# A decoder trunk on one core: decay scores in four-way steps, attention heads in pairs, small columns in the first block, memory tokens split four tiles after their load

## The chip, the core and the metric

The kernel runs on one core of one Trainium2 chip. The core has TensorE (PE, matrix products into PSUM), VectorE (DVE), ScalarE (ACT), GpSimd (POOL) and SyncE (SP, which issues the transfers here). Weights come from the chip's main memory through the core's 16 DMA engines. The metric is the device time of one execution in microseconds: the median of several runs. One further execution was profiled, and all rows below are from it.

## What is computed

One layer over 256 tokens of width 2048, in float32. Cut to what matters here:

```python
h = rmsnorm(x, norm_gain); z = h @ w_in            # one projection, split into all of the below
# A) gated linear attention, 4 heads, keys 128 wide, values 256 wide, chunks of 64
gk_log = log_sigmoid(gdown @ w_gk_up + b_gk) / 16   # gdown: 16 columns of z
b = cumsum(gk_log)                                  # log decay, per key channel
scores[i, j] = sum_d q[i, d] * k[j, d] * exp(b[i, d] - b[j, d])      for j <= i
o_a = rmsnorm(scores @ v + carried state) * silu(ggate)
# B) forgetting attention, 8 heads of 64; c = cumsum(log_sigmoid(flogit + b_f)), 8 columns of z
p = softmax(q.k / 8 + c_t - c_s, for s <= t);       o_b = (p @ v) * silu(fgate)
# C) attention into 256 memory tokens, 4 heads of 128, from rmsnorm(mem) @ w_mem_kv
o_c = softmax(q.mem_k / sqrt(128)) @ mem_v * silu(mgate)
y = sum over the branches of sigmoid(merge_b) * (o_b @ w_branch_b)
out = rmsnorm(x + y @ w_out, final_gain)
```

## The kernel before

**The main stream.** All weights are cut into 34 blocks of 512 columns in the order in which they are used. A block has 16 k-tiles of 128 rows. Float32 products are made from split operands: `split_w` (L123 to 125) casts a raw tile to a rounded `hi` on ScalarE (L124) and subtracts on VectorE to get `lo` (L125), and the activations are split in the same way (L256, L257). A block is then either `natural` (tokens in rows, L166 to L168: three products of 512 columns per k-tile and token half) or `transposed` (channels in rows, L187 with 512 columns and L189 with 256, four such pairs per k-tile). Weights arrive in quarters of four k-tiles (1 MB) in `raw` tiles, of which there are three; `hi` and `lo` have four buffers of two k-tiles each.

**The order of the work.** The orders of TensorE and of SP are those of the program. The orders on VectorE, ScalarE and GpSimd are made by a planner when the kernel is built; it takes work that its own costs say is ready, the weight splits first (`tc.high_priority(AHEAD)`), and else by place in the program. The attention work is written as generators: after each k-tile (in `transposed` after each of the four column groups, which comes to as many) `pull()` lets the side lane and the main lane go on; a `yield n` means n such tiles until the next piece. The main lane holds, one after another, `small_and_norm`, `gla_decay`, `gla_scores`, `gla_out`, `fox` and `memory`; the side lane loads and splits the memory tokens (`load_mem`).

**The first block** (`first_w`, L279 to 300) loads activations and weights in small pieces and is `transposed` with one k-tile at a time into four banks of the `att` pool (128 x 512 floats, four banks; `acc` is the other pool of four).

**The small columns.** The 16 gate columns and the 8 forget columns (`wsm`, L340) are laid into 128-column tiles `zs` after the first block, and sixteen products of 512 columns (L386) follow in `small_and_norm`, within the second block.

**The decay scores.** exp(b_i - b_j) is made finite by a reference point between j and i. For each level s in 64, 32, 16, 8, 4, 2, 1 a 128-token tile is cut into blocks of s; the keys of an even block and the queries of the odd block behind it are scaled against the last row of the even block (`prep`: two differences L453 and L454, one exponential L455, two products L457 and L460). Eight products of 64 columns per level (L495) go to one bank, are multiplied by a mask (L497) and added into the scores `gA` (L500); the next level follows 11 tiles later. The diagonal comes first from products of all keys with all queries (L477) and a scaled identity. The products across the two token tiles are in L485.

**The heads of the forgetting attention** run through `staged(8, (scores, trans, values), (0, 2, 3), 3)`: one head per stage every three tiles. `values` (L589 to 596) multiplies with 64 columns of weights, for even heads into rows 0 to 63 of a bank and for odd heads into rows 64 to 127; two banks are held for all eight heads.

Of the kernel before, what the change touches and what calls it, by code (L numbers as in the profile page):

```python
# [16 lines left out]
P = 128  # L17
S = 256
# [34 lines left out]
LEVEL_GAP = 11  # L53
N_WARM = 8
LEVELS = (64, 32, 16, 8, 4, 2, 1)
# [4 lines left out]
def body(ctx, tc, xT, memT, xn, memn, wall, wsm, wup, cst, fgain, out):  # L60
# [93 lines left out]
    def h_of(h, kt):  # L154
        return h[kt // 4][:, kt % 4]
# [116 lines left out]
    def load_mem():  # L272
        for g in range(4):
            m12.append(new_h("m12_", g))
            raw = wpool.tile([P, 4, S], F32, tag="raw", name=nm("raw"), bufs=3)
            load_split(memT, "m12_", C_MGAIN, g, m12[g], raw, slice(0, 4))
            yield 6

    def first_w():  # L279

        wb = w_block()
        for g in range(4):
# [5 lines left out]
            for s in range(2):  # L288
# [28 lines left out]
    def scale_T(r, row):  # L317
        nc.vector.tensor_tensor(out=r, in0=r, in1=row.unsqueeze(1).to_broadcast([P, 4, S]), op=ALU.mult)
        return r
# [19 lines left out]
    wsr = cpool.tile([P, KT, 24], F32, name="wsr")  # L339
    nc.sync.dma_start(wsr, wsm)  # L340
    wup_s = cpool.tile([16, 512], F32, name="wup_s")
    nc.sync.dma_start(wup_s, wup)

    gmask = cpool.tile([P, len(LEVELS), 64], F32, name="gmask")
    nc.gpsimd.memset(gmask, QS)
    for li, s in enumerate(LEVELS):
        nb = 64 // s
        mk_ = gmask[:, li, :].rearrange("p (b s) -> p b s", s=s)
        nc.gpsimd.affine_select(out=mk_, in_=mk_, pattern=[[-2 * s, nb], [0, s]],
                                compare_op=ALU.is_ge, fill=0.0, base=0, channel_multiplier=1)  # L350
        nc.gpsimd.affine_select(out=mk_, in_=mk_, pattern=[[2 * s, nb], [0, s]],
                                compare_op=ALU.is_ge, fill=0.0, base=s - 1, channel_multiplier=-1)
    gdiag = cpool.tile([P, P], F32, name="gdiag")
    nc.vector.tensor_scalar(gdiag, ident, QS, None, ALU.mult)
# [8 lines left out]

    zs = []
    for g in range(2):
        z0 = a4([P, 8, P], F32)
        nc.gpsimd.memset(z0, 0.0)
        ws = a4([P, 8, P], F32R)
        wr = wsr[:, 8 * g:8 * g + 8, :]
        nc.vector.tensor_copy(ws, z0)  # L370
        for (a, b, wdt) in ((0, 0, 16), (32, 16, 8)):
            nc.vector.tensor_copy(ws[:, :, a:a + wdt], wr[:, :, b:b + wdt])
            nc.vector.tensor_tensor(out=ws[:, :, 64 + a:64 + a + wdt], in0=wr[:, :, b:b + wdt],
                                    in1=ws[:, :, a:a + wdt].bitcast(F32), op=ALU.subtract)
        zs.append(ws)
    sm = cpool.tile([64, S], F32, name="sm")

    def small_and_norm():
# [5 lines left out]
        sp = att()  # L384
        for kt in range(KT):
            MM(sp, lhsT=zs[kt // 8][:, kt % 8, :], rhs=h_of(x12, kt).rearrange("p a s -> p (a s)"),  # L386
               start=(kt == 0), stop=(kt == KT - 1))
        yield from norm
        yield from row_of(xcol, xrow)
        scale_T(G["q"], xrow)  # L390
        scale_T(G["k"], xrow)
        nc.scalar.copy(sm, sp[0:64, S:])
        nc.vector.tensor_tensor(out=sm, in0=sp[0:64, :S], in1=sm, op=ALU.add)
        nc.vector.tensor_tensor(out=sm, in0=sp[64:128, :S], in1=sm, op=ALU.add)
# [47 lines left out]
    def gla_scores():  # L442
# [3 lines left out]

        def prep(s):
            nb = 1024 // (2 * s)
            Bv = gB.rearrange("p (b u s) -> p b u s", u=2, s=s)
            E = a4([P, 1024])  # L450
            Ev = E.rearrange("p (b u s) -> p b u s", u=2, s=s)
            ref = Bv[:, :, 0, s - 1:s].to_broadcast([P, nb, s])
            nc.vector.tensor_tensor(out=Ev[:, :, 0, :], in0=ref, in1=Bv[:, :, 0, :], op=ALU.subtract)  # L453
# [475 lines left out]
```

## Time and profile before

| | |
|---|---|
| median of 3 runs | 824.55 us (824.29 to 824.95) |
| the profiled execution | 824.89 us, of it the span 823.2 us |
| granted TensorE clock, mean | 0.997 |
| busy: PE, PEld, DVE, ACT, POOL | 98%, 83%, 60%, 50%, 2% |
| transfers | 157.15 MB, 191 GB/s on average |

The span runs from the first to the last instruction. Busy shares are averages over stages with different loads. Products are pipelined, so the duration of one (0.39 us for 512 columns) is longer than the distance from one start to the next (0.23 us), and what work costs TensorE is read from starts. A float32 product of the attention work, whose operands are not split, runs as two passes and counts twice in the number of instructions.

### The profile page before, as it was taken

How to read it: one execution, taken by the hardware profiler on the slowest of the kernel's cores; microseconds unless marked ns; L12 is line 12 of the kernel's file. 1: busy time of each engine (PE TensorE's matmuls, PEld its weight loads, DVE VectorE, ACT ScalarE, POOL GpSimd, SP SyncE). 2: the span in 40 equal slices, each digit the busy share in tenths (PEclk: the TensorE clock that was granted, in tenths of full speed). 3: DMA queues.
4: the chain of work that ended last, by engine and by line, in shares of the span. 5: the costliest groups of instructions: out<-in, count | busy, mean ns of one | idle time of the engine just before them, and what ended most of it. 6: DMA issues, size and time to landing. Idle time of an engine off the chain costs nothing.

```text
span 823.2 us, 10033 instructions
## 1 busy us (share of the span) xinstructions
PE 809.6 (98%) x3958; PEld 679.4 (83%) x3958; DVE 497.6 (60%) x657; ACT 408.4 (50%) x547; POOL 15.4 (2%) x36
## 2 busy tenths in 40 slices
PE   8999999999999999999999999999999999999995
PEld 7888888888888778888888888888888888888885
DVE  6755988875647667567445744475446544566833
ACT  7746755743454456455444444444444444445611
POOL 4000100000000000000000000000000000000000
PEclk9999999999999999999999999999999999999998
DMA  8943466844534344445555545554555455576803
GB/s 302 385 176 125 155 228 230 300 158 169 189 140 168 108 148 154 148 160 199 182 187 199 205 170 192 200 204 167 191 205 202 166 195 205 199 266 249 307 0 103
DMA packets 27359, 157.15 MB, mean 191 GB/s; under 512 B 3216, under 2 KB 4640, under 8 KB 10416
## 3 DMA queue, kind: packets, MB, share of 16 engines
q1 hardware_dynamic: 27040, 156.48, 53.3%
q8 instruction: 31, 0.51, 0.2%
q14 instruction: 16, 0.13, 0.0%
q10 hardware_dynamic: 144, 0.02, 0.0%
q0 software_dynamic: 128, 0.02, 0.0%
HBM read 154.39 MB, written 2.10 MB: 190 GB/s over the span
## 4 chain that ended last, share of the span: by engine, by line
PE 90%; DVE 3%; DMA 2%; ACT 2%; issue 1%; SPq 1%; POOL 0%; DVEq 0%; ACTq 0%; POOLq 0%
PE acc L166 18%; PE acc L168 18%; PE acc L167 18%; PE acc L187 12%; PE acc L189 6%; PE acc L822 4%; PE acc L821 4%; PE acc L820 4%; DMA raw<-wall 1%; PE att L495 1%; DMA raw<-memT 1%; PE att L187 1%; DVE lo L125 1%; ACT hi L124 1%; PE att L593 1%
## 5 line engine op out<-in xcount | busy, mean ns | idle before, releaser
L125 DVE TENSOR_TENSOR lo<-raw,hi 128x1024 fp32r<-128x1024 f32 (+2 forms) x269 | 321.0, 1203 | 248.4 <-ACT hi L124 248.0
L124 ACT CAST hi<-raw 128x1024 fp32r<-128x1024 f32 (+2 forms) x269 | 275.3, 1035 | 291.1 <-PE acc L168 215.2
L166 PE MATMUL acc<-hi,x 128*128 128x512 f32 x544 | 215.3, 396 | 0.0
L168 PE MATMUL acc<-hi,x 128*128 128x512 f32 x544 | 212.0, 390 | 0.0
L167 PE MATMUL acc<-lo,x 128*128 128x512 f32 x544 | 211.8, 389 | 0.0
L187 PE MATMUL acc<-x,hi 128*128 128x512 f32 x384 | 137.2, 400 | 1.1 <-ACT a L327 1.1
L168 PEld LDWEIGHTS acc<-hi,x 128*128 128x128 f32 x544 | 102.1, 188 | 21.7
L166 PEld LDWEIGHTS acc<-hi,x 128*128 128x128 f32 x544 | 102.2, 188 | 21.2 <-issue 0.5
L167 PEld LDWEIGHTS acc<-lo,x 128*128 128x128 f32 x544 | 102.2, 188 | 20.5
L189 PE MATMUL acc<-x,lo 128*128 128x256 f32 x384 | 107.3, 280 | 0.0
L187 PEld LDWEIGHTS acc<-x,hi 128*128 128x128 f32 x384 | 72.1, 188 | 18.1 <-ACT a L327 1.6
L189 PEld LDWEIGHTS acc<-x,lo 128*128 128x128 f32 x384 | 72.4, 189 | 0.3
L166 PE MATMUL acc<-hi,oT 128*128 128x512 f32 x128 | 49.8, 389 | 0.0
L167 PE MATMUL acc<-lo,oT 128*128 128x512 f32 x128 | 49.8, 389 | 0.0
L168 PE MATMUL acc<-hi,oT 128*128 128x512 f32 x128 | 49.8, 389 | 0.0
L820 PE MATMUL acc<-hi,a 128*128 128x512 f32 x96 | 37.5, 391 | 0.0
L822 PE MATMUL acc<-hi,a 128*128 128x512 f32 x96 | 37.4, 389 | 0.0
L821 PE MATMUL acc<-lo,a 128*128 128x512 f32 x96 | 37.4, 389 | 0.0
L167 PEld LDWEIGHTS acc<-lo,oT 128*128 128x128 f32 x128 | 24.0, 188 | 5.0
L168 PEld LDWEIGHTS acc<-hi,oT 128*128 128x128 f32 x128 | 24.0, 188 | 5.0
L166 PEld LDWEIGHTS acc<-hi,oT 128*128 128x128 f32 x128 | 24.0, 188 | 5.0
L187 PE MATMUL att<-x,hi 128*128 128x512 f32 x64 | 23.4, 406 | 0.5 <-ACT hi L124 0.5
(215 smaller groups left out, 781.3 us busy)
## 6 DMA issues: line engine op xcount, KB each, us to landing
raw<-wall SPq DMA_DIRECT2D x132, 1024.0 KB, 4.7
a<-xn SPq DMA_DIRECT2D x8, 512.0 KB, 8.5
raw<-wall SPq DMA_DIRECT2D x4, 512.0 KB, 7.2
raw<-memT SPq DMA_DIRECT2D x4, 512.0 KB, 4.2
raw<-memn SPq DMA_DIRECT2D x4, 512.0 KB, 4.6
out<-a SPq DMA_DIRECT2D x8, 256.0 KB, 3.3
raw<-wall SPq DMA_DIRECT2D x7, 256.0 KB, 4.9
a<-xT SPq DMA_DIRECT2D x8, 128.0 KB, 4.2
```

The source lines that it names most:

```text
L124: nc.scalar.copy(hi, src)
L125: nc.vector.tensor_tensor(out=lo, in0=src, in1=hi.bitcast(F32), op=ALU.subtract)
L166: MM(ps[t], lhsT=h1, rhs=hi, start=(kt == first), stop=False)
L167: MM(ps[t], lhsT=h1, rhs=lo, start=False, stop=False)
L168: MM(ps[t], lhsT=h2, rhs=hi, start=False, stop=(kt == last))
L187: MM(ps[c], lhsT=hi[:, cs_], rhs=hk.rearrange("p a s -> p (a s)"), start=(kt == 0), stop=False, skip_group_check=True)
L189: MM(ps[c][:, :S], lhsT=lo[:, cs_], rhs=hk[:, 0, :], start=False, stop=(kt == KT - 1), skip_group_check=True)
L495: MM(ps[:, e, :], lhsT=E[:, e * P:(e + 1) * P], rhs=Q[:, e, :], start=True, stop=True)
L593: MM(o, lhsT=fv[:, 0, hs], rhs=pt[:, :S], start=True, stop=False, skip_group_check=True)
L820: MM(ps, lhsT=h1, rhs=hi, start=(kt == 0), stop=False)
L821: MM(ps, lhsT=h1, rhs=lo, start=False, stop=False)
L822: MM(ps, lhsT=h2, rhs=hi, start=False, stop=(kt == KT - 1))
```

## The change

- `gla_scores` has steps of 32, 8 and 2 in place of seven levels. In a step a block of 4s tokens is cut into four parts; each part of keys is scaled against its own end, and for each of the first three parts the later queries of the block are scaled against that end: (3+2+1) x 32 = 192 columns a tile. So a step takes two levels' worth of pairs, with eight products of 192 columns over four banks, and its results are copied into `gA` under a mask (`copy_predicated`) and not added. A last step of the same size takes neighbours (64 columns) and, with the plain queries (128 columns), the diagonal. Steps are 18 tiles apart. Queries get their factor QS when they are scaled by `xrow`.
- `fox` takes two heads at a time: the values of a pair go to one bank of their own, with the passes of the two heads side by side, and the stages are written out with two or three tiles between.
- The small columns are loaded and laid out behind the first group of the first block, and their products stand in that block behind the second, third and fourth group, into a bank of `acc`. The copy of zeros moves to GpSimd.
- The memory tokens of a group are split four tiles after their transfer is issued; the next group still follows six tiles after it.
- The warm-up has six products, not eight.

```diff
-LEVEL_GAP = 11
-N_WARM = 8
-LEVELS = (64, 32, 16, 8, 4, 2, 1)
+STEP_GAP = 18
+N_WARM = 6
+STEPS = (32, 8, 2)
+Q_OFF = (0, 96, 160)
+Q_N = 192
...
             raw = wpool.tile([P, 4, S], F32, tag="raw", name=nm("raw"), bufs=3)
-            load_split(memT, "m12_", C_MGAIN, g, m12[g], raw, slice(0, 4))
-            yield 6
+            nc.sync.dma_start(raw, memT[:, 4 * g:4 * g + 4, :])
+            yield 4
+            for k in range(4):
+                kt = 4 * g + k
+                split_x(m12[g], raw[:, k, :], k, cs[:, C_MGAIN + kt:C_MGAIN + kt + 1])
+            yield 2
...
+    def small_w():
+        nc.sync.dma_start(wsr, wsm)
+        for g in range(2):
+            z0 = a4([P, 8, P], F32)
+            nc.gpsimd.memset(z0, 0.0)
+            ws = a4([P, 8, P], F32R)
+            wr = wsr[:, 8 * g:8 * g + 8, :]
+            nc.gpsimd.tensor_copy(ws, z0)
+            for (a, b, wdt) in ((0, 0, 16), (32, 16, 8)):
+                nc.vector.tensor_copy(ws[:, :, a:a + wdt], wr[:, :, b:b + wdt])
+                nc.vector.tensor_tensor(out=ws[:, :, 64 + a:64 + a + wdt], in0=wr[:, :, b:b + wdt],
+                                        in1=ws[:, :, a:a + wdt].bitcast(F32), op=ALU.subtract)
+            zs.append(ws)
+    sp = acc()
+    def small_mm(kts):
+        for kt in kts:
+            MM(sp, lhsT=zs[kt // 8][:, kt % 8, :], rhs=h_of(x12, kt).rearrange("p a s -> p (a s)"),
+               start=(kt == 0), stop=(kt == KT - 1))
...
+            if g == 0:
+                small_w()
+            else:
+                small_mm(range(0 if g == 1 else 4 * g, 4 * g + 4))
...
         def prep(s):
...
+            E = a4([P, 1024])
+            Bv = gB.rearrange("p (b s) -> p b s", s=s)
+            nc.vector.tensor_tensor(out=E.rearrange("p (b s) -> p b s", s=s),
+                                    in0=Bv[:, :, s - 1:s].to_broadcast([P, 1024 // s, s]), in1=Bv,
+                                    op=ALU.subtract)
             nc.scalar.activation(E, E, AF.Exp, scale=1.0 / 16)
             nc.vector.tensor_tensor(out=E, in0=E, in1=gkf, op=ALU.mult)
+            for half in range(2):
+                Q = a4([P, 4, Q_N])
+                for b in range(3):
+                    w, nb = (3 - b) * s, 32 // s
+                    end = blocks(gB, half, 4 * s)[:, :, (b + 1) * s - 1:(b + 1) * s]
+                    nc.vector.tensor_tensor(
+                        out=of_q(Q, b, s), in0=later(gB, half, b, s),
+                        in1=end.rearrange("p (e b) s -> p e b s", e=4).to_broadcast([P, 4, nb, w]),
+                        op=ALU.subtract)
+                nc.scalar.activation(Q, Q, AF.Exp, scale=1.0 / 16)
+                for b in range(3):
+                    nc.vector.tensor_tensor(out=of_q(Q, b, s), in0=of_q(Q, b, s),
+                                            in1=later(gqf, half, b, s), op=ALU.mult)
+                Qs.append(Q)
+            return E, Qs
...
-        for c in range(2):
-            ps = att()
-            for e in range(4):
-                sl = slice((4 * c + e) * P, (4 * c + e + 1) * P)
-                MM(ps[:, e * P:(e + 1) * P], lhsT=gkf[:, sl], rhs=gqf[:, sl], start=True, stop=True)
...
-            yield 3
-        nxt = prep(LEVELS[0])
+        nc.gpsimd.memset(gA, 0.0)
+        yield 6
+        nxt = prep(STEPS[0])
         yield 8
...
+        for li in range(len(STEPS) + 1):
+            E, Qs = nxt
+            if li < len(STEPS):
+                nxt = prep(STEPS[li + 1]) if li + 1 < len(STEPS) else prep_pairs()
+            for c in range(4):
+                ps = att()[:, :2 * Q_N].rearrange("p (a b) -> p a b", a=2)
+                for j in range(2):
+                    e = 2 * c + j
+                    MM(ps[:, j, :], lhsT=E[:, e * P:(e + 1) * P], rhs=Qs[c // 2][:, e % 4, :],
+                       start=True, stop=True)
...
+                for dst, mask, src in parts:
+                    nc.vector.copy_predicated(
+                        dst, mask.bitcast(U32).unsqueeze(1).to_broadcast(list(src.shape)), src)
+            yield STEP_GAP
...
-            o = po[h // 4][64 * (h % 2):64 * (h % 2) + 64, (h // 2) % 2, :]
-            MM(o, lhsT=fv[:, 0, hs], rhs=pt[:, :S], start=True, stop=False, skip_group_check=True)
-            MM(o[:, P:], lhsT=fv[:, 1, hs], rhs=pt[:, S:], start=False, stop=True, skip_group_check=True)
...
+        def values(p):
+            po = att()
+            for a, b, j, sl in ((0, S, 0, slice(0, S)), (P, S, 1, slice(S, 3 * P))):
+                for e in range(2):
+                    h = 2 * p + e
+                    MM(po[64 * e:64 * e + 64, a:b], lhsT=fv[:, j, h * 64:(h + 1) * 64], rhs=pts[h][:, sl],
+                       start=(j == 0), stop=(j == 1), skip_group_check=True)
+            nc.scalar.copy(ob[:, p, :], po[:, :S])
+        for k in range(6):
+            if k >= 2:
+                values(k - 2)
+                yield 2
+            if 1 <= k < 5:
+                for e in range(2):
+                    trans(2 * (k - 1) + e)
+                yield 2
+            if k < 4:
+                for e in range(2):
+                    scores(2 * k + e)
+                yield 3
```

More of the change, by code (lines that the diff above doesn't have):

```diff
@@ L315, in plain_T, with scale_T @@
         return r
-    def scale_T(r, row):
-        nc.vector.tensor_tensor(out=r, in0=r, in1=row.unsqueeze(1).to_broadcast([P, 4, S]), op=ALU.mult)
+    def scale_T(r, row, by=1.0):
+        nc.vector.scalar_tensor_tensor(out=r, in0=r, scalar=by, in1=row.unsqueeze(1).to_broadcast([P, 4, S]),
+                                       op0=ALU.mult, op1=ALU.mult)
         return r
@@ L361, in body @@
                                 base=0, channel_multiplier=1)
[L364 to L375, printed above, removed]
     sm = cpool.tile([64, S], F32, name="sm")
+    nc.scalar.copy(sm, sp[0:64, S:])
+    nc.vector.tensor_tensor(out=sm, in0=sp[0:64, :S], in1=sm, op=ALU.add)
+    nc.vector.tensor_tensor(out=sm, in0=sp[64:128, :S], in1=sm, op=ALU.add)
     def small_and_norm():
@@ L383, in small_and_norm @@
             yield next(norm)
[L384 to L387, printed above, removed]
         yield from norm
         yield from row_of(xcol, xrow)
-        scale_T(G["q"], xrow)
+        scale_T(G["q"], xrow, QS)
         scale_T(G["k"], xrow)
-        nc.scalar.copy(sm, sp[0:64, S:])
-        nc.vector.tensor_tensor(out=sm, in0=sp[0:64, :S], in1=sm, op=ALU.add)
-        nc.vector.tensor_tensor(out=sm, in0=sp[64:128, :S], in1=sm, op=ALU.add)
         nc.vector.tensor_tensor(out=sm, in0=sm, in1=xrow[0:64], op=ALU.mult)
@@ L445, in gla_scores, with blocks, of_q, later @@
         B4 = gB.rearrange("p (h t i) -> p h t i", h=4, t=2)
+        def blocks(x, half, s):
+            return x[:, 512 * half:512 * half + 512].rearrange("p (b s) -> p b s", s=s)
+        def of_q(Q, b, s):
+            w = (3 - b) * s
+            return Q[:, :, Q_OFF[b]:Q_OFF[b] + 32 * (3 - b)].rearrange("p e (b s) -> p e b s", s=w)
+        def later(x, half, b, s):
+            v = blocks(x, half, 4 * s)[:, :, (b + 1) * s:]
+            return v.rearrange("p (e b) s -> p e b s", e=4)
         def prep(s):
-            nb = 1024 // (2 * s)
@@ new lines, in prep, with prep_pairs @@
+            return E, Qs
+        def prep_pairs():
+            Qs = []
+            for half in range(2):
+                Q = a4([P, 4, Q_N])
+                Bh, qh = blocks(gB, half, 2), blocks(gqf, half, 2)
+                odd = Q[:, :, :64]
+                pick = lambda v, u: v[:, :, u].rearrange("p (e b) -> p e b", e=4)
+                nc.vector.tensor_tensor(out=odd, in0=pick(Bh, 1), in1=pick(Bh, 0), op=ALU.subtract)
+                nc.scalar.activation(odd, odd, AF.Exp, scale=1.0 / 16)
+                nc.vector.tensor_tensor(out=odd, in0=odd, in1=pick(qh, 1), op=ALU.mult)
+                nc.gpsimd.tensor_copy(Q[:, :, 64:], gqf[:, 512 * half:512 * half + 512].rearrange(
+                    "p (e i) -> p e i", e=4))
+                Qs.append(Q)
+            return gkf, Qs
@@ L556, in fox @@
         ob = G["ob"] = a4([P, 4, S])
-        po = [att().rearrange("p (c s) -> p c s", c=2) for _ in range(2)]
         sums = cpool.tile([P, 8, NT], F32, name="fsum")
```

74 lines of the change are left out of this document (29 added, 45 removed).

## The prediction, made before the changed kernel was run

> **What bounds the kernel now.** I read the engine totals and the share of the chain first, then the waits of TensorE, then its timeline wherever its own starts show a hole, and last the engines that feed it.
>
> ```profile
> PE 809.6 (98%) x3958; PEld 679.4 (83%) x3958; DVE 497.6 (60%) x657; ACT 408.4 (50%) x547; POOL 15.4 (2%) x36
> PE 90%; DVE 3%; DMA 2%; ACT 2%; issue 1%; SPq 1%; POOL 0%; DVEq 0%; ACTq 0%; POOLq 0%
> ...
> 17.86 0.39 PE L187 MATMUL att<-x,hi 128*128 128x512 f32 x1
> 18.97 0.39 PE L189 MATMUL att<-x,lo 128*128 128x256 f32 x1 [0.72 <-DVE lo L125]
> ...
> 109.30 0.28 PE L189 MATMUL acc<-x,lo 128*128 128x256 f32 x1
> 110.73 0.50 PE L187 MATMUL acc<-x,hi 128*128 128x512 f32 x1 [1.15 <-ACT a L327]
> ...
> 329.20 0.60 PE L626 MATMUL att<-ident,b 128*128 128x128 f32 x4
> 330.55 0.70 PE L612 MATMUL att<-a,a 128*128 128x256 f32 x2 [0.75 <-ACT b L616]
> ```
>
> The rows of the timeline give start, duration and, in brackets, the idle time and who ended it. TensorE is never without work except at the two ends and in three holes. Taken from start to start, against about 0.23 us from an L187 to its L189, 0.12 us from an L189 to the next L187 and 0.44 us for four transposes, they are 0.9, 1.3 and 0.9 us. So time falls almost one for one with TensorE's own instructions, and the stalls that can still be removed come to 3.1 us. A change on VectorE, ScalarE or a queue counts only where it makes or fills such a hole. The sum below is made against the profiled execution, 824.89 us (span 823.2, and 1.7 around it); the runs' median is 0.34 below that, less than a measurement of this kernel can tell from no change, which is about 0.2% or 1.65 us.
>
> **Part 1: four-way decay steps (TensorE).**
>
> ```profile
> 73.24 0.39 PE L168 MATMUL acc<-hi,x 128*128 128x512 f32 x1
> 73.47 1.05 PE L477 MATMUL att<-a,a 128*128 128x128 f32 x8
> 74.28 0.48 PE L166 MATMUL acc<-hi,x 128*128 128x512 f32 x1
> ...
> 99.11 0.39 PE L168 MATMUL acc<-hi,x 128*128 128x512 f32 x1
> 99.34 1.89 PE L495 MATMUL att<-b,a 128*128 128x64 f32 x16
> 101.04 0.48 PE L166 MATMUL acc<-hi,x 128*128 128x512 f32 x1
> ...
> 227.70 0.59 PE L514 MATMUL att<-a,b 128*128 128x256 f32 x2
> 228.13 0.59 PE L515 MATMUL att<-a,a 128*128 128x256 f32 x2
> ```
>
> Each fp32 product runs as two passes, hence x8 for four and x16 for eight. A pass of 64 columns takes 1.70/16 = 0.106 us, one of 128 columns 0.81/8 = 0.101, one of 256 columns 0.43/2 = 0.215. So up to 128 columns the price is flat and then it doubles. A batch costs its passes and about 0.09 us at its edge (the next L166 is 0.48 long, not 0.39). Before: two diagonal batches of 0.90 and seven levels of 1.79, together 14.3 us. After: four batches (32, 8, 2, pairs) of eight products with 192 columns, 16 passes each. The trace has no pass of 192 columns. At the price of 128 columns a batch is 1.7 us, at that of 256 it is 3.5, so the gain lies between 7.4 and 0.1 us. I take the middle by columns, 0.16 us a pass: 2.65 a batch, 10.6 in all, a gain of **3.7 us**, since 192 lies halfway between two measured sizes on the stretch where columns are paid for.
>
> **Part 2: heads in pairs.**
>
> ```profile
> 261.25 0.40 PE L168 MATMUL acc<-hi,x 128*128 128x512 f32 x1
> 261.58 0.65 PE L593 MATMUL att<-b,a 128*64 128x256 f32 x2
> 262.06 0.38 PE L594 MATMUL att<-b,a 128*64 128x128 f32 x2
> 262.37 0.55 PE L585 MATMUL att<-ident,b 128*128 128x128 f32 x3
> ```
>
> One head's values hold TensorE 0.10 us before their first start (0.33 against 0.23) and 0.79 us after it: 0.9, of which the four passes are 2 x 0.215 + 2 x 0.108 = 0.65; the other 0.25 is going to the 64-column shape and back. Eight heads: 7.2 us. In pairs the way there and back is paid four times, not eight. If the passes of the two heads run one after another, a pair is 1.30 + 0.25 and the gain is 1.0 us. If the second head, which writes the other 64 rows of the bank, costs nothing, a pair is 0.9 and the gain is 3.6. No row here shows two neighbours of different halves; since a head's two passes must follow each other and only what stands beside them can overlap, I take the middle, **2.3 us**. Scores and transposes are as many as before.
> The Trainium skill, "TensorEngine Tiling (Array Packing)", Key Properties, says that different tiles load weights and multiply in parallel and that a change of the tiling mode drains the array. The 0.25 us above agrees with the drain; by its first half alone the gain would be 3.6 us, and no run so far shows that for fp32's two passes.
>
> **Part 3: small columns within the first block.**
>
> ```profile
> 49.24 0.28 PE L189 MATMUL acc<-x,lo 128*128 128x256 f32 x1
> 49.36 3.83 PE L386 MATMUL att<-x,a 128*128 128x512 f32 x16
> 53.03 0.39 PE L187 MATMUL acc<-x,hi 128*128 128x512 f32 x1
> ...
> 11.37 0.69 DVE L125 TENSOR_TENSOR lo<-raw,hi 128x512 fp32r<-128x512 f32 x1 [0.61 <-ACT hi L124]
> ...
> 34.83 0.33 DVE L372 CAST a<-wsr 128x128 fp32r<-128x128 f32 x2
> 35.09 0.43 DVE L373 TENSOR_TENSOR a<-wsr,a 128x128 fp32r<-128x128 f32 x2
> ...
> 7.25 1.85 POOL L367 MEMSET a<- 128x1024 f32 x2
> ...
> 10.00:15.00 5.00, 5.00 (x30) 4.34 (x29) 4.38 (x9) 4.24 (x9) 0.00 (x0) 1.00 1.01 349
> ```
>
> The sixteen products cost 3.67 us wherever they stand. Eight of them now stand ahead of the ninth k-tile, which is where the hole at 17.86 is (the 33rd pair of L187 and L189, four to a k-tile): 1.8 us of work covers its 0.9. Against that, the small weights' transfer (197 KB) is now issued ahead of the second group's loads, while the queues are full at 349 GB/s (the last number of the window from 10 to 15), so those land 0.6 us later; and eight small VectorE operations (1.3 us by the rows of L372 and L373) stand among splits that TensorE takes just in time (the split at 11.37 ends at 12.06, its product starts at about 12.2). The ends are a gain of 0.9 and a loss of 0.9; I take a gain of **0.3 us**. The full-tile copy leaves VectorE for GpSimd (at most two tiles, about 1 us each by the memset), long before anybody waits. Two warm-up products fewer free TensorE earlier, but its first operand is not ready earlier: nothing.
> The Trainium skill, "GPSIMD Engine Reference", section 1, says that GpSimd shares its SBUF interfaces with VectorE and contends with VectorE instructions of two SBUF inputs, which speaks against moving copies there; the splits that ran beside the memset (0.69 us) were no longer than the one at 11.37, but a memset reads nothing. By the rule this part would lose up to 2 us instead.
>
> **Part 4: the first step (a new wait).**
>
> ```profile
> 82.00:99.30 17.30, 16.94 (x19) 1.00 0.45 153
> ...
> 84.69 2.29 DVE L432 TENSOR_TENSOR_SCAN a<-a,a 128x1024 f32<-128x1024 f32 x1
> ...
> 92.38 0.68 DVE L453 TENSOR_TENSOR a<-a 128x512 f32<-128x512 f32 x1
> 92.98 0.69 DVE L454 TENSOR_TENSOR a<-a 128x512 f32<-128x512 f32 x1
> 93.58 1.22 DVE L125 TENSOR_TENSOR lo<-raw,hi 128x1024 fp32r<-128x1024 f32 x1
> 94.72 0.68 DVE L453 TENSOR_TENSOR a<-a 128x512 f32<-128x512 f32 x1
> ...
> 97.66 1.21 DVE L460 TENSOR_TENSOR a<-a,a 128x1024 f32<-128x1024 f32 x1
> ```
>
> The window row is VectorE alone: 98% busy between 82 and 99.3. From start to start 512 elements take 0.60 us and 1024 take 1.14, so 0.07 fixed and about 1 ns an element. The first level's E was ready at about 98.8, and TensorE came at 99.34: half a microsecond to spare. After the change TensorE comes there 1.8 us earlier (no diagonal) and 0.3 by part 3: 97.2. Between the scan's end (87.0) and its first half VectorE has the cross-tile products (1.8), E twice (2.3) and three differences and three products of the first half (0.46 + 0.33 + 0.20, twice: 2.0), 6.1 us; one weight split of 1.14 in every 2.7 us leaves it 58%, so this is done at 97.5, the second half at 101.0. TensorE needs the latter 1.3 us after the former: 98.8. I take a wait of **2.0 us**; the ends are 0 (the second half's differences fill gaps while ScalarE exponentiates) and 4.0 (they do not, and the exponentials stand in line). Behind the waiting product stands the whole weight stream.
> Later steps have 25 us of lead. Over all steps VectorE's work is unchanged: 7 x 4.14 + 1.2 = 30.2 us before; after, 3 x (2.3 + 4.0 + 2.4) + 3.4 = 29.5, with the masked copies, which no row shows, at VectorE's price for other operations; at twice that, 6 us more.
>
> **Part 5: memory tokens.**
>
> ```profile
> 94.83 0.33 SPq L262 DMA_DIRECT2D raw<-memT  x1
> ...
> 104.53 0.33 SPq L262 DMA_DIRECT2D raw<-memT  x1
> 106.23 7.00 SPq L129 DMA_DIRECT2D raw<-wall  x2
> ...
> 108.79 1.31 ACT L256 ACTIVATE m<-raw,cs 128x256 fp32r<-128x256 f32 x3 [2.95 <-DMA raw<-memT]
> ```
>
> ScalarE stood 2.95 us before a transfer, and the eviction L327 queued behind it is what TensorE waited for at 110.73. A split that comes four tiles later finds its data. But only TensorE's and SP's orders are written out; ScalarE's is a planner's, so a later place in the program is a lower rank and not a fixed time. Of the 1.3 us I count **0.8**; the ends are 0 and 1.3. The 0.9 us at 330.55 lie where memory attention meets the gates' work; with 5 tiles fewer for the decay steps and 5 fewer for the heads memory attention starts earlier: **0.3** of 0.9.
>
> Sum: 824.9 - 3.7 - 2.3 - 0.3 + 2.0 - 0.8 - 0.3 = **819.6 us**.
>
> **Rivals.** (a) Everything helps: heads overlap, no wait at the first step, all holes gone: 824.9 - 3.7 - 3.6 - 3.1 = 814.5. For it: VectorE's total does not grow. Against: its 98% just there.
> (b) The change does not do what it says in two places: the heads do not overlap, and the planner splits the memory tokens when it did before: 819.6 + 1.3 + 0.8 = 821.7.
> (c) VectorE becomes the bound from 87 to 150: the masked copies cost twice their elements, 1.6 us more in each of two steps that fall in that stretch, and the first wait is 4.0: 819.6 + 3.2 + 2.0 = 824.8, no change.
> (d) The raw buffers, slower than before.
>
> ```profile
> raw<-wall SPq DMA_DIRECT2D x132, 1024.0 KB, 4.7
> ```
>
> There are three, and the issues from 94.83 to 106.23 came as one was freed. A memory tile held four tiles longer keeps its buffer 4 x 1.39 = 5.6 us more (1.39 for four pairs of L187 and L189), and the weight load behind it in SP's order comes as much later. The second load of the row at 106.23 was issued by 113.2 and landed 4.7 later by the page's median, at 117.9; it is the fourth quarter of the block that begins at 110.73, due 3 x 5.56 later at 127.4, less 3.3 for its casts and splits: 6.2 us to spare. If the next step's VectorE work, 8.7 us in place of a level's 4.1, goes ahead of the split, the hold grows by 10.2 and each of two loads misses by 4.0: 819.6 + 8.0 = 827.6. It decides from 6.2 us of added hold. Against: a planner may split the tokens as they land.
>
> **How the numbers follow.** Forecast 0.45, (a) 0.12, (b) 0.17, (c) 0.13, (d) 0.13. The forecast's own range is 817 to 821.5. Faster by over 0.2% (under 822.9) is the forecast, (a), (b), less a little for the near side of (b): 0.72. (c) is within 0.2%, with that little: 0.15. (d) is slower: 0.13. The range runs from (a) to just past (c), 814.5 to 826: it leaves out (d) and the far side of (a), under 0.2.
>
> **What would show it.** Part 1: four batches of about 2.65 us in place of seven of 1.79. Part 2: four value batches, 0.9 to 1.55 us each. Part 3: no hole at the ninth k-tile, perhaps one near the fifth. Part 4: a TensorE wait for VectorE at the first 192-column batch. Part 5: ScalarE's waits for memT (8.8 us in all before) mostly gone and no wait of TensorE for lo or hi between 95 and 150. The forecast is wrong if TensorE's waits between 87 and 150 sum to over 5 us, or if a 192-column pass costs that of 256.

## The result and the profile after

| | before | after |
|---|---|---|
| median of four runs each | 824.62 us (824.29 to 824.95) | 829.62 us (828.84 to 830.96) |
| ratio to before, 95% interval | | 1.0062 [1.0045, 1.0080] |
| the profiled execution | 824.89 us, span 823.2 | 830.96 us, span 829.1 |
| granted TensorE clock, mean | 0.997 | 0.994 |

The changed kernel is slower by 5 us, 0.6%, where 819.6 us was forecast with a range to 826. First the engines' busy time and the shares of the chain, on the page of after:

```profile
PE 807.0 (97%) x3890; PEld 675.0 (81%) x3890; DVE 497.2 (60%) x700; ACT 407.9 (49%) x551; POOL 21.8 (3%) x46
...
PE 84%; DVE 7%; DMA 4%; ACT 3%; issue 1%; SPq 0%; POOL 0%; DVEq 0%; ACTq 0%; POOLq 0%
```

TensorE does less and the run takes longer: its share of the chain fell from 90% to 84%, VectorE's rose from 3% to 7%, that of the transfers from 2% to 4%. VectorE's sum is the same, 497.2 us against 497.6, in 700 instructions and not 657. Then the waits of TensorE in after (line waited for, us in total, times, longest; line numbers are shifted by 3 in this part of the code, so L190 and L192 are the old L187 and L189):

```profile
PE acc L190 <- ACT hi L127: 2.5, 2, 1.9
PE acc L192 <- DVE lo L128: 2.2, 5, 0.8
PE att L553 <- ACT m L259: 1.8, 1, 1.8
...
PE acc L170 <- DVE lo L128: 1.0, 1, 1.0
```

Most of it is waiting for split weights, `hi` and `lo`, for which TensorE waited in before only in the first block, 0.72 us at the longest. The row of L553 names the memory split L259 on ScalarE, which ended at 99.92; but the six products L503 on VectorE (98.82, below) make that batch's queries, the third of them ended at 99.90, and TensorE's own wait for VectorE at 99.94. So this is the wait for VectorE of Part 4. The places stand in TensorE's timeline of after:

```profile
97.82 0.39 PE L171 MATMUL acc<-hi,x 128*128 128x512 f32 x1
100.05 2.84 PE L553 MATMUL att<-a,a 128*128 128x192 f32 x16 [1.84 <-ACT m L259]
...
154.49 0.28 PE L192 MATMUL acc<-x,lo 128*128 128x256 f32 x1
156.63 0.49 PE L190 MATMUL acc<-x,hi 128*128 128x512 f32 x1 [1.87 <-ACT hi L127]
157.89 0.58 PE L192 MATMUL acc<-x,lo 128*128 128x256 f32 x1 [0.77 <-DVE lo L128]
158.27 0.63 PE L190 MATMUL acc<-x,hi 128*128 128x512 f32 x1
...
193.56 2.76 PE L553 MATMUL att<-a,a 128*128 128x192 f32 x16
196.03 0.52 PE L190 MATMUL acc<-m,hi 128*128 128x512 f32 x1
196.39 0.28 PE L192 MATMUL acc<-m,lo 128*128 128x256 f32 x1
...
262.47 0.87 PE L662 MATMUL att<-b,a 128*64 128x256 f32 x8
263.27 0.50 PE L190 MATMUL acc<-x,hi 128*128 128x512 f32 x1
...
310.46 0.33 PE L733 MATMUL att<-ident,a 128*128 128x128 f32 x1 [1.45 <-DVE a L750]
```

From start to start, against the prices that the prediction used, I counted every gap over 0.2 us beyond its price, each from its start to the next start; so the gap at 97.8 is 2.0 us where the row's idle time says 1.84. Up to the last product the kernel after is 5.5 us later, made up so:

| | before | after |
|---|---|---|
| TensorE's own work: steps -3.9, pairs -3.1 | | -7.0 us |
| first 95 us | 2.6 | 2.6 |
| at the first step (97.8) | 0 | 2.0 |
| other gaps from 95 to 170 | 1.3 | 8.4 |
| gaps after 170 | 0.9 | 2.6 |
| products at half clock (158.3 to 160.8: four pairs of L190 and L192 take 2.56 us, not 1.41) | 0 | 1.15 |

The profiled execution is the slowest of the four. The half clock is not the cause of the loss: the execution with the mean clock of before, 0.997, took 828.84 us. The rest, about half a microsecond, is made of gaps under 0.2 us, which were not counted, rounding, and the start, where the pairs take 0.64 us and not 0.35 until 7.2 us after and until 6.0 before. So the savings came, and what has to be found is the cause of the 7 us more between 95 and 170.

**Where it comes from.** Back from the late splits to the casts, which wait for weights. ScalarE in after:

```profile
118.90 2.00 ACT L127 CAST hi<-raw 128x1024 fp32r<-128x1024 f32 x2 [5.19 <-DMA raw<-wall]
...
155.53 1.99 ACT L127 CAST hi<-raw 128x1024 fp32r<-128x1024 f32 x2 [3.57 <-DMA raw<-wall]
```

And from there to the queue that issues the loads, in order, on SP. After, and below it one row of before (its other issues stand in the prediction):

```profile
94.64 0.33 SPq L279 DMA_DIRECT2D raw<-memT  x1
98.92 0.33 SPq L132 DMA_DIRECT2D raw<-wall  x1
105.95 0.33 SPq L279 DMA_DIRECT2D raw<-memT  x1
114.01 2.98 SPq L132 DMA_DIRECT2D raw<-wall  x2
118.24 0.33 SPq L279 DMA_DIRECT2D raw<-memT  x1
...
125.78 0.33 SPq L279 DMA_DIRECT2D raw<-memT  x1
132.99 8.77 SPq L132 DMA_DIRECT2D raw<-wall  x2
143.44 1.91 SPq L218 DMA_DIRECT2D raw<-memn  x2
150.66 0.33 SPq L132 DMA_DIRECT2D raw<-wall  x1
```

```profile
100.04 0.33 SPq L129 DMA_DIRECT2D raw<-wall  x1
```

After, no weight load is issued from 98.92 to 114.01. Before, three were in that time: at 100.04 and the two of the row at 106.23. From 105.95 on two of the three raw buffers hold memory tokens. The row at 114.01 ends at 116.99 because its second load had to wait for the first of these buffers, so that was held from 94.64 to about 116.6, 22 us. Its first load waited for the third buffer, the weights of 98.92, whose last split ended at 113.98.

The same happens once more, and there it costs more (5.4 us of gaps from 146.5 to 158, against 0.8 at 120 to 122). The third and fourth memory tiles (118.24 and 125.78) are held 25 and 19 us, until the memory norm's loads of 143.44 and 145.0 take their buffers; in before no memory tile was held over 9.7. So from 125.78 on the weights go through one buffer, one quarter at a time (122.37, then 132.99 and 141.4 in one row), and the next weights, of 150.66, stand behind the norm's loads; the cast at 155.53 waits for them. What held the memory tiles is VectorE, in after:

```profile
98.82 2.09 DVE L503 TENSOR_TENSOR a<-a,a 128x384 f32<-128x384 f32 x6
100.83 1.22 DVE L486 TENSOR_TENSOR a<-a 128x1024 f32<-128x1024 f32 x1
...
107.38 2.10 DVE L503 TENSOR_TENSOR a<-a,a 128x384 f32<-128x384 f32 x6
109.40 0.37 DVE L567 COPY_PREDICATED a<-gmask,att 128x192 f32<-128x192 uint32 x1
...
114.83 0.48 DVE L260 SCALAR_TENSOR_TENSOR m<-raw,cs,m 128x256 fp32r<-128x256 f32 x1
...
115.36 2.85 DVE L260 SCALAR_TENSOR_TENSOR m<-raw,cs,m 128x256 fp32r<-128x256 f32 x7
...
142.13 2.86 DVE L260 SCALAR_TENSOR_TENSOR m<-raw,cs,m 128x256 fp32r<-128x256 f32 x7
```

and in before:

```profile
99.93 0.48 DVE L257 SCALAR_TENSOR_TENSOR m<-raw,cs,m 128x256 fp32r<-128x256 f32 x1
...
103.60 0.87 DVE L257 SCALAR_TENSOR_TENSOR m<-raw,cs,m 128x256 fp32r<-128x256 f32 x2
```

Before, VectorE put the four splits of the first memory tile (L257) between the pieces of a level and was done at 104.5. After, the preparation of the next step (L486 to L503) and the masked copies of the first (L567) stand ahead of them, and L260 begins at 114.83. The third and fourth tiles are split mostly at 142.13, behind the third step's preparation and the second step's masked copies. How full VectorE is there shows in the windows of after (length, then busy time of PE, PEld, DVE, ACT and POOL, the granted clock, the share of the DMA engines, GB/s):

```profile
95.00:110.00 15.00, 13.16 (x66) 11.13 (x65) 15.00 (x32) 9.44 (x14) 1.63 (x2) 1.00 0.43 141
...
155.00:160.00 5.00, 2.60 (x8) 2.07 (x9) 2.48 (x3) 4.18 (x6) 0.00 (x0) 0.74 0.60 206
```

VectorE is busy for all 15 us from 95 to 110. Its total over the run did not grow, but it comes in lumps, and the transfers stand behind them. Up to here this is read from one trace; the runs below test it.

### The profile page after: what moved, and what is told of

Its sections match the earlier page's. It is cut to its first block, busy times and chain, and to the rows that moved or that the text cites. A ratio compares the mean times of both kernels' runs of the same rounds, so it can differ in the third digit from the quotient of the medians.

```text
span 829.1 us, 9961 instructions
## 1 busy us (share of the span) xinstructions
PE 807.0 (97%) x3890; PEld 675.0 (81%) x3890; DVE 497.2 (60%) x700; ACT 407.9 (49%) x551; POOL 21.8 (3%) x46
## 4 chain that ended last, share of the span: by engine, by line
PE 84%; DVE 7%; DMA 4%; ACT 3%; issue 1%; SPq 0%; POOL 0%; DVEq 0%; ACTq 0%; POOLq 0%
PE acc L169 18%; PE acc L170 18%; PE acc L171 18%; PE acc L190 9%; PE acc L192 5%; PE acc L902 4%; PE acc L901 4%; PE acc L900 4%; DMA raw<-wall 3%; DVE lo L128 2%; PE att L190 1%; ACT hi L127 1%; DMA raw<-memn 1%; PE att L192 1%; DMA raw<-memT 0%
## 5 line engine op out<-in xcount | busy, mean ns | idle before, releaser
L128 DVE TENSOR_TENSOR lo<-raw,hi 128x1024 fp32r<-128x1024 f32 (+2 forms) x269 | 321.1, 1204 | 262.5 <-ACT hi L127 262.2
L127 ACT CAST hi<-raw 128x1024 fp32r<-128x1024 f32 (+2 forms) x269 | 275.1, 1035 | 297.6 <-PE acc L171 220.9
L190 PE MATMUL acc<-x,hi 128*128 128x512 f32 x384 | 138.7, 403 | 3.2 <-ACT hi L127 2.5
L192 PE MATMUL acc<-x,lo 128*128 128x256 f32 x384 | 108.9, 284 | 2.2 <-DVE lo L128 2.2
L190 PEld LDWEIGHTS acc<-x,hi 128*128 128x128 f32 x384 | 72.7, 189 | 20.8 <-ACT hi L127 3.1
L192 PEld LDWEIGHTS acc<-x,lo 128*128 128x128 f32 x384 | 73.2, 191 | 4.1 <-DVE lo L128 3.8
L190 PE MATMUL att<-x,hi 128*128 128x512 f32 x64 | 24.1, 414 | 1.0 <-DVE x L260 1.0
```

Of the source, the lines that this page charges most:

```text
L127: nc.scalar.copy(hi, src)
L128: nc.vector.tensor_tensor(out=lo, in0=src, in1=hi.bitcast(F32), op=ALU.subtract)
L190: MM(ps[c], lhsT=hi[:, cs_], rhs=hk.rearrange("p a s -> p (a s)"), start=(kt == 0), stop=False, skip_group_check=True)
L192: MM(ps[c][:, :S], lhsT=lo[:, cs_], rhs=hk[:, 0, :], start=False, stop=(kt == KT - 1), skip_group_check=True)
```

## The experiments

These theories were set against each other. H: the late place of the memory split holds the raw buffers. D: the four-way steps' VectorE work, in lumps, holds them, wherever the split stands. F: the damage is elsewhere, in the first-step wait or the heads. Their rival in the expectations is V: the lumps on VectorE cost time whatever the memory tokens do. Gaps are counted as above, from one profiled execution each, and so is the last column, the length of the stretches at half clock between the first 10 us and the last product. That execution can lie off the median (827.71 us for the split at once, 820.72 for the last of the kernels with loads spread). The ratios are to the kernel before, run on the same chip.

| | median us | ratio [95%] | gaps 95 to 170 | gaps after 170 | at half clock, us |
|---|---|---|---|---|---|
| after | 829.62 | 1.0062 [1.0045, 1.0080] | 10.4 | 2.6 | 3.4 |
| after, split at once | 829.09 | 1.0057 [1.0036, 1.0078] | 8.1 | 2.6 | 0 |
| after, late split ranked first | 830.81 | 1.0075 [1.0060, 1.0090] | 8.7 | 2.6 | 10.2 |
| after, memory tokens 16 tiles later | 824.28 | 0.9991 [0.9981, 1.0001] | 2.0 | 4.7 | 0 |
| after, own buffers | 827.05 | 1.0030 [1.0020, 1.0040] | 4.1 | 2.6 | 0 |
| after, first step 3 tiles later | 830.91 | 1.0069 [1.0052, 1.0087] | 12.9 | 0 | 6.8 |
| after, loads spread | 822.83 | 0.9971 [0.9958, 0.9985] | 2.1 | 2.4 | 3.4 |
| after, loads and gates spread | 823.63 | 0.9981 [0.9965, 0.9997] | 3.7 | 0 | 0 |
| before + late split | 825.91 | 1.0010 [1.0000, 1.0019] | 1.7 | 0.9 | 0 |
| before + pairs | 827.79 | 1.0035 [1.0022, 1.0048] | 1.2 | 6.2 | 3.4 |
| before + steps | 833.36 | 1.0101 [1.0085, 1.0116] | 8.6 | 2.9 | 3.4 |
| before + steps, memory tokens 16 tiles later | 828.94 | 1.0049 [1.0030, 1.0067] | 2.0 | 6.9 | 6.8 |
| before + small columns | 825.51 | 1.0005 [0.9994, 1.0015] | 1.2 | 0.9 | 0 |

**The late split taken back.** After, with the old call:

```diff
-            nc.sync.dma_start(raw, memT[:, 4 * g:4 * g + 4, :])
-            yield 4
-            for k in range(4):
...
-            yield 2
+            load_split(memT, "m12_", C_MGAIN, g, m12[g], raw, slice(0, 4))
+            yield 6
```

> The changed kernel with the memory tokens split right behind their load's issue again, six tiles to the next; nothing else undone. Theory H (the memory tiles hold the three raw buffers too long, so the weight loads queued behind them on SP come late, and TensorE starves between 146 and 168 us): of the 9 us of TensorE holes there nearly all go, and the time is 819 to 822 us. Rival V (the larger VectorE bursts of the decay steps delay the weight splits whatever the memory tokens do): the holes move, and it stays at 826 to 830. Both leave the wait of about 2 us at the first decay step.

It is as slow as after: 829.09. The first weight loads are late by the same amount. The issues on SP in this run, and below them one row of TensorE:

```profile
99.14 0.33 SPq L132 DMA_DIRECT2D raw<-wall  x1
...
114.12 2.98 SPq L132 DMA_DIRECT2D raw<-wall  x2
```

```profile
137.37 0.47 PE L190 MATMUL acc<-x,hi 128*128 128x512 f32 x1 [1.87 <-ACT a L346]
```

Again 15 us without a weight load, and the first memory tile held 22 us. H falls. Behind that the run differs: the third tile is held 9 us and not 25, the gaps from 146.5 to 158 shrink to 1.0 us, and 2.0 us stand at 135 in their place. That gap is not for weights. TensorE waits for the eviction of a block (L346, L347), whose VectorE part at 136.80 stands behind the masked copies of 135.35 (1.54 us). So lumps on VectorE also cost time in a second way, without the raw buffers.

**The late split alone**, the other way round: the same lines in before.

> The kernel before with only the memory tokens' split moved four tiles behind the load's issue. Theory H in its plain form (four tiles of hold are enough): 3 to 8 us slower than before, 828 to 832. Theory H in its other form (the hold grows only because the decay steps' VectorE work stands ahead of the split): within 1.5 us of before, or up to 1.3 us faster because the hole at 110 us goes.

825.91, +0.1%, less than the measurement tells from no change. The hole of 1.3 us at 109.3 stays, 1.2 here. So the late place alone costs at most 1.6 us (the interval's upper end), and it does not bring the 0.8 of Part 5 either. The first memory tile is held 9.7 us, as in before.

**The late split ranked first.** After, with the memory split among the work that the planner takes first:

```diff
-                split_x(m12[g], raw[:, k, :], k, cs[:, C_MGAIN + kt:C_MGAIN + kt + 1])
+                with tc.high_priority(AHEAD):
+                    split_x(m12[g], raw[:, k, :], k, cs[:, C_MGAIN + kt:C_MGAIN + kt + 1])
```

> The changed kernel with the memory tokens' split at its late place, but taken by the planner at the weight splits' rank. Theory H: what counts is when the split is done and the buffer is free, not where it stands in the program, so this is within 1.5 us of the variant that splits at once (819 to 822 us). Rival: the late place itself binds (TensorE's or SP's order waits for it), and it stays at 826 to 830.

830.81, a miss. The hold itself is cured, and the time is not:

```profile
100.84 0.33 SPq L279 DMA_DIRECT2D raw<-memT  x1
106.26 2.40 SPq L132 DMA_DIRECT2D raw<-wall  x2
```

```profile
PE acc L190 <- DVE a L352: 3.6, 1, 3.6
```

The first tile's buffer is free after 6.3 us (94.54 to 100.84), none is held over 10.1, the weight loads come in time, and no gap is left from 142 to 170. But the gap at the first step grew from 2.0 to 4.0 us, behind the memory split that now goes first, and one of 3.7 came at 138, at an eviction (L352) behind masked copies and weight splits on VectorE. The granted clock was at half twice, for 10.2 us in all. With VectorE full from 95 to 110, an order by rank only chooses who waits: the lumps are the cause, and the raw buffers are the way by which they cost most in after, but not the only way. V holds in part.

**The steps alone** in before (all of `gla_scores` and the masks from the change, nothing else).

> The kernel before with only the four-way decay steps. The variants so far have taken theory H in its plain form away: splitting at once left 829.1 us and the late split alone cost 0.9. Theory D: the steps' VectorE work, put together in lumps of about 9 us, stands ahead of the memory tokens' split on VectorE, so their raw buffers are held 21 us and not 10 and the weight loads behind them on SP come late. Then the steps alone make the holes between 98 and 168 us (about 8 us) against 3.7 us less work on TensorE: 827 to 830. Rival (the holes need the pairs or the small columns too): 821 to 824.

833.36: the steps by themselves cost 8.7 us, more than the whole change. The issues on SP are those of after:

```profile
98.83 0.33 SPq L132 DMA_DIRECT2D raw<-wall  x1
...
113.93 2.97 SPq L132 DMA_DIRECT2D raw<-wall  x2
```

This run splits the memory tokens right behind their load, as before did. The part that lengthened the hold (22 us again) is therefore the steps: D. Of its 8.6 us of gaps, 1.9 are the first step's and 2.0 the eviction at 135, as in the run that splits at once.

**The memory tokens later.** After, with `side.append(gap(16))` ahead of `load_mem`, so that their loads begin 16 tiles later; work and buffers are the same.

> The changed kernel with the side lane held back by 16 tiles, so that the memory tokens are loaded some 22 us later, behind the first two steps' lumps. Theory D: the weight loads keep their place, the holes between 110 and 160 shrink from 8 us to under 4, and the time is 822 to 826. Rival (VectorE alone is too slow for the steps there, whatever is loaded): 828 to 831.

824.28, 5.3 us less than after: the one line takes back the whole loss (0.9991 of before, an interval of 0.9981 to 1.0001). Its SP rows:

```profile
88.65 25.14 SPq L132 DMA_DIRECT2D raw<-wall  x5
118.95 0.33 SPq L279 DMA_DIRECT2D raw<-memT  x1
```

Five weight loads run through the first two steps' lumps, which are as they were, so V in its plain form falls too. Of the gaps from 95 to 170 only the first step's 2.0 us is left. Some of the collision moved: 2.1 us appear at 180, where TensorE waits for weights whose load SP issued at 175.29, behind the loads of the memory norm (L218), which take the same buffers.

**Own buffers.** After, with the memory tokens in two buffers of their own (tag `rawm`), loaded at the same place of the program. Two small tiles (`wsr`, `wup_s`) moved to another pool to make room.

> The changed kernel with two buffers of their own for the memory tokens, so that they never hold one of the three raw buffers (two small weight tiles move into the common pool of activations to make room). Theory D: no weight load waits for a memory split until the third group, whose load waits for the first group's split; holes between 110 and 160 under 4 us, 822 to 826. Rival (VectorE alone): 828 to 831.

827.05, the gaps from 95 to 170 down from 10.4 to 4.1. Weight loads go out at 98.08, 102.36 and, in the same row, by 109.7. But a new gap of 2.9 us stands at 33.5, at the end of the first block, behind the small columns' products; I put it down to the moved tiles, without a run that shows it. If it counts in full, the run without it would be at 824, an estimate. Of the 4.1 us, 1.9 are the first step's and 2.2 stand at 139 to 143, the larger part again at an eviction on VectorE (L351). Taken with the run before it: where the memory tokens' work may come late, the shared buffer is what costs. Where it is put ahead, as in the run ranked first, it costs elsewhere.

**Steps in before, memory tokens 16 tiles later.**

> The kernel before with only the decay steps, and the side lane held back by 16 tiles. Theory D: the steps' loss (833.4 us alone) is nearly all in the weight loads queued behind the held memory buffers, so it comes down by 7 to 10 us, to 823 to 826. Rival (what the whole change gained from the later memory tokens came through the pairs' earlier stages): over 829.

828.94: against the kernel before on the same chip +3.7 us, where the steps alone cost +8.7, so the later memory tokens bring 5.0. But it is not the 823 to 826 expected, and just short of the rival's 829. The gaps from 95 to 170 are again the 2.0 alone. What is left lies after 170, with two stretches at half clock behind it: 2.8 us at the memory-norm loads from 180.7, and this, in TensorE's waits:

```profile
PE acc L190 <- DVE b L719: 2.8, 1, 2.8
```

It is the eviction of a gate's block, and the steps alone have it too. ScalarE in the run with the steps alone shows what it stood behind:

```profile
329.61 0.47 ACT L669 ACTIVATE b<-att,mmx 128x256 f32<-128x256 f32 x1 [2.75 <-DVE mmx L667]
...
330.65 1.28 ACT L718 ACT_TABLE_LOAD   x1
331.94 1.26 ACT L718 ACTIVATE b<-acc,xcol 128x512 f32<-128x512 f32 x2
```

The gate's first operation on ScalarE (L718) is behind a head's exponential of memory attention, which waited 2.75 us for VectorE, and behind a table load of 1.28. Memory attention now comes a few tiles earlier and meets the block's end. In after it comes earlier still and meets another point (308.7: 1.6 us). No run moves memory attention by itself, so this is read from the traces.

**Pairs alone** in before (`fox` from the change).

> The kernel before with only the heads in pairs. The changed kernel's trace shows a pair's value batch at 1.03 us, against 7.2 us for eight heads before: 3.1 us less work for TensorE. Theory: 821 to 822 us, less what the moved memory attention meets (one new wait of up to 1.6 us near the gates' work), so 821 to 823.5. Rival (pairs save nothing because fewer tiles between the stages make TensorE wait for transposed probabilities): 824 to 826.

827.79, slower by 2.7 us, a miss of both expectations. The pair's products are as short as in after, but the eviction of the block behind them is late. TensorE in this run:

```profile
262.51 0.87 PE L594 MATMUL att<-b,a 128*64 128x256 f32 x8
265.77 0.47 PE L166 MATMUL acc<-hi,x 128*128 128x512 f32 x1 [2.39 <-DVE a L314]
```

Two heads' softmax work stands in one lump on VectorE and ScalarE, the casts and splits of the next weights behind it, and the eviction L314 behind those. The second gap, 2.9 us at 326, is the gate's eviction of the run above: pairs alone, like steps alone, move memory attention onto that spot, and both together move it past. So the parts do not add: +8.7 (steps), +2.7 (pairs), +0.9 (late split) and +0.3 us (small columns), each against the kernel before on the same chip, are 12.6, and together they are 5.0.

**Small columns alone** in before, with the six warm-up products.

> The kernel before with only the small columns in the first block and six warm-up products. Theory: the sixteen products cost 3.67 us in either place, the hole of 0.9 us at the ninth k-tile is covered and one or two of 0.6 to 1.0 us open earlier: 824 to 826 us. Rival (a gain, as the forecast had it): under 824.

825.51, no difference. The hole at 17.86 is gone, and two of 0.8 us stand at 5.9 and 11.9 in its place. The one at 11.9 waits for both parts of an activation split, which end together (12.69 on ScalarE, 12.68 on VectorE, there behind the eight small operations). The one at 5.9 waits for VectorE's part alone (L257). Here is GpSimd, VectorE and TensorE of this run:

```profile
5.37 1.04 POOL L290 CAST a<-a 128x1024 fp32r<-128x1024 f32 x1
```

```profile
5.52 1.16 DVE L257 SCALAR_TENSOR_TENSOR x<-a,cs,x 128x256 fp32r<-128x256 f32 x1 [0.40 <-ACT x L256]
```

```profile
6.83 0.47 PE L187 MATMUL att<-x,hi 128*128 128x512 f32 x1 [0.64 <-DVE x L257]
```

The split takes 1.16 us beside GpSimd's full-tile copy, where the other fifteen of the block take 0.47 to 0.49. In after the second split takes 1.29 us beside the same copy.

**The first step later.** After, with 3 tiles more ahead of the first step (`yield 6` for `yield 3`).

> The changed kernel with the first step three tiles (about 4 us) later. All theories: the wait of 2.0 us at the first step, which is for the second and third stage of its operands on VectorE, goes. What differs: if the hole is worth its size, the time is 827 to 828.5; if TensorE only waits elsewhere in its place, because VectorE is the bound of the whole stretch, it stays at 829 to 831.

830.91, no gain. The 2.0 us at the first step are gone, and the other gaps up to 170 are larger by 4.5 in sum (12.9 against 8.4). Its longest waits are one of 2.9 us for an eviction (L365), one of 2.5 for `lo` (L128) and one of 2.1 for `hi` (L127); the clock was at half for 6.8 us. As long as the weights come late here, taking away a wait ahead of them gains nothing: TensorE only stands later. F falls for the first step.

**Loads spread.** After, with what the runs pointed to: memory tokens 12 tiles later, the memory norm's loads 5 tiles apart, not 2, and the first step 3 tiles later.

```diff
-                yield 2
+                yield apart
...
-        yield 3
+        yield 6
...
+    side.append(gap(12))
```

> The changed kernel with the side lane held back by 12 tiles, its four loads for the norm of the memory tokens five tiles apart and not two, and the first decay step three tiles later. Theory D: with the weight loads in time, a hole at the first step (2.0 us) is worth its size, though it was not while they were late, and the 2.1 us at the block of memory keys go too: 819 to 822 us. Rival (VectorE is the bound of the stretch, holes only move): 823.5 to 826.

822.83 (821.16 to 825.56, ten runs): faster than both kernels, by 0.3% than before, but between the 819 to 822 expected and the rival's 823.5. The first step's 2.0 us are gone and an eviction at 109 (L365) waits 2.0 in their place; 2.4 us are left at 181, at the block of memory keys. Three edits stand in this run at once, so what each is worth is not shown.

**Loads and gates spread**: the same, and the gates' transposes 7 tiles apart, not 4.

> As the one before, and the transposes behind the first gate blocks wait seven tiles and not four. Theory: the hole of 1.6 us at the first of them (TensorE waits for VectorE's gate product) goes and nothing takes its place: 1 to 1.6 us under the one before, 818 to 821. Rival (memory attention's table loads on ScalarE open it elsewhere): the same as the one before within 0.5 us.

823.63: not told apart from the run above, and not the 818 to 821 expected, though the gaps after 170 are gone. The eviction at 109 (2 us) is in both and stays open.

## Why the prediction was wrong

- **Part 1, TensorE's steps: right.** A batch is 2.60 us (2.47 to the next start, 0.13 at its edge) against 2.65, a pass of 192 columns 2.47/16 = 0.154 us against 0.16.
- **Part 2, pairs: the mechanism right, its size too small.** Eight passes take 0.80 us where one after another would take 1.30, so the second head costs 0.15 us: a pair is 1.02 us with going there and back, 7.2 to 4.1, a gain of 3.1 and not 2.3. The Trainium skill's rule ("TensorEngine Tiling (Array Packing)", Key Properties) that tiles multiply in parallel, by which it would be 3.6, was nearer than the middle that I took. What Part 2 left out are the lumps: it costed no VectorE or ScalarE work of two heads at once, and alone the pairs lose 2.7 us.
- **Part 3, small columns: right within what can be measured**, 0 where 0.3 was taken, and the exchange was the one named: the ninth k-tile's hole against earlier ones. "GPSIMD Engine Reference", section 1, of the Trainium skill names contention between GpSimd and VectorE instructions with two SBUF inputs, and the trace agrees: the split beside GpSimd's copy took 1.16 us, some 0.7 more, and made one of the two new holes. The 2 us that Part 3 put on it as the most did not come: that run is at 1.0005 of before. The prediction looked for it beside a memset and left it out of its sum.
- **Part 4, the first step: its size was right, 2.0 us, in part by luck.** It put the first half's queries at 97.5 and let TensorE wait for the second half, at 101.0. Measured, the first half came at 99.90, so the whole wait is there, and the second half at 100.91, in time for its product at 101.10.
- **The step that failed is the sentence behind Part 4**, "Later steps have 25 us of lead. Over all steps VectorE's work is unchanged". Both halves hold for the scores. Neither says when VectorE's other work is done. In a stretch where VectorE was known to be 98% busy, the work was costed by its sum, and its grain, some 9 us at a time in place of 4, was used only in a rival. So the sum has no term for memory tiles held behind the steps (22, 25 and 19 us, where none was over 9.7) nor for late evictions; measured, that is 7 us more of gaps between 95 and 170 and 1.15 us at half clock.
- **Part 5, the memory tokens: ScalarE's waits for memT went from 8.8 to 0.6 us, as forecast**, but the run gained nothing from it alone (825.91): TensorE's hole at 109.3 went from 1.3 to 1.2 us there, and to 0.85 in after.
- **The 0.3 at 330.55**: that hole went, and the one at 308.7, 1.6 us, came. Which of them one gets hangs on where memory attention meets a gate block's end, and was not worked out.
- **Rival (d)**, given 0.13, is the nearest to what happened. It said that a hold decides from 6.2 us more, and put 5.6 on the late place and 4.6 on the step's work ahead of the split. The first tile's hold grew from 9.7 us (94.83 to 104.5) to 22. With the late place taken back it is the same, so its first half was worth next to nothing and its second half was undersized: ahead of the split stood a whole preparation and the masked copies of the step before (100.8 to 114.8). Nor does it have the third and fourth tiles, where most of the time went. Its 827.6 was short by 2.0, and came near partly by luck: the half clock (1.15) and the gates' gap at 308.7 (1.6) were not in it, and its 8 us stand at two loads that did not cost so much. Its argument against itself, that a planner may split the tokens as they land, is what the row at 114.83 contradicts.
- The forecast's own test, TensorE's waits between 87 and 150 over 5 us, comes out at 5.8.
- **The sum** as written gives 819.5, not 819.6, which changes nothing.

Left open: why the planner put the step's work ahead of the memory splits even where these came right behind their load; and how much of the 828.94 belongs to the memory-norm loads and how much to the gates, which only the two runs with the loads spread touch, with several edits at once.

## What to carry to other kernels

That the sum of an off-path engine's work does not grow is no cover when the work comes in fewer, larger lumps. List what else stands in that engine's order inside each lump, which buffers it holds, and which in-order queue allocates from them: here the weight stream starved through that chain with no engine full on average. Where two streams share a small set of buffers, hold the unhurried one back past the lump; here that single line was worth 5.3 us, all that the change had cost. A higher rank for it was worth nothing, since it only moved the wait. And savings measured alone and taken together differed here, because each moved a later stage against a block's end.

## What the runs showed of the hardware

Two fp32 products on the two halves of 64 columns overlap almost fully, 0.80 us for eight passes that would cost 1.30 in a row (twice the 0.65 of one head). A masked copy out of PSUM costs about what other VectorE operations do (192 elements: 0.26 us from start to start, 109.40 to 109.66). A VectorE split with two SBUF operands took 1.16 and 1.29 us beside a GpSimd cast, 0.48 otherwise.

The clock falls for less than I had thought. In the second window row of after above, 155 to 160, the granted clock is 0.74 (the third number from the end). That is half clock from about 157.4 on, and it ends at 160.8, where the pairs of L190 and L192 go from 0.64 us back to 0.35: 3.4 us. In the 3.4 us ahead of 157.4 TensorE had worked 0.8 and stood 2.6, in two holes, counted from starts at the prices above. The 2.0 us gap at 97.8 alone did not bring the clock down. The clock records of the traces put these stretches on a fixed grid: each lasts 3.41 us or twice that, and within a run their beginnings lie whole multiples of 3.413 us apart (157.41 and 823.01 in after: 195). Counted on that grid over all the profiled executions, the nine stretches just ahead of a fall within the run held 2.0 to 3.3 us of idle time, and behind the first 10 us no other stretch at full clock ahead of the last product held more than 2.0. The gap at 97.8 lies across two stretches, 1.3 and 0.7 us. The Trainium skill ("TensorE: Matmul & The Clock Gate", What's actually happening) puts the fall after at least one idle window of about 3.4 us; the length of the slow stretch agrees, while here 2.6 us of idle time within such a stretch were enough.
